# A streaming-encoder block on one core: a ring of small tiles made 64 bytes wider, and the tiles behind it moved

## The chip, the core and the metric

The kernel runs on one core of a Trainium2 chip. The metric is the device time of one execution in microseconds (us); the time before is the median of 3 runs. A duration in nanoseconds is marked ns. The engines are named as in the profile: PE is TensorE (PEld its weight loads), DVE is VectorE, ACT is ScalarE, POOL is GpSimd and SP is SyncE, which only issues transfers.

## What is computed

One layer of an encoder on 256 tokens of width 2048, in float32:

```
x += 1/2 * SwiGLU(norm(x))                  # ffn1: 2048 -> 2 x 5632 -> 2048
h  = norm(x); proj = h @ w_in               # HGRN2, RG-LRU, gates
x += (sig(gate_A) * y_A + sig(gate_B) * y_B) @ w_out
x += CrossAttention(norm(x), norm(mem))     # 4 heads, 256 memory tokens
x += 1/2 * SwiGLU(norm(x))                  # ffn2
out = norm(x)
```

## The kernel before, in words

All large products are done on PE with each operand split in two float32r halves: a high part `h` and a low part `l` of a weight piece, and a high and a low part of the activations. ACT makes the high part (`split`, lines 578 to 580: a copy), DVE the low part (a subtraction). In the two feed-forward stages, ffn1 and ffn2, most products are formed by a scheme of seven products of half-size blocks (`PRODUCTS`, line 1005), for which DVE also makes sums of weight blocks (`td`, `sums_into`) that are split again into a second `h` and a `tl`.

A product of 512 columns is a matmul whose stationary operand (128 columns, loaded into the array before) is a piece of the activations, and whose moving operand is a block of 512 columns of a weight tile. In the profile such a matmul is written `acc<-h,ms`: the moving tile first (`h`, `l`, `tl`), then the stationary one (`ms`, `xh`, `xl`, `xd`, `hidop`, `ops`). In `product` (line 755) of the middle stage it is the other way round, `acc<-ops,h`. Each matmul has its own weight load.

Weight pieces are transferred by SP into tiles of 128 x 2048 float32 (8,192 bytes in each partition). The same kind of tile holds the raw piece, the high and low parts and the sums. There is one ring of them, `big`: ten places that exist for the whole program, and in ffn1 and ffn2 four more from the pool `more` (`FFN_POOLS`, line 870), so 14 places. Between ffn1 and ffn2 the room of these four is used by pools of smaller tiles (`tmp`, `tmp2`, `bias`, `scores`, `extra`, `feature`). The activations' operands stand in 22 tiles of 128 x 1024 (`slots`, 4,096 bytes in each partition). At the start of ffn1 the stationary operands `ms` of the memory's values (`BigOperands`, line 1240) also stand in tiles of the big ring.

A recording layer (`Flow`) takes all operations down, and a planner (`arrange`) sets, from its own table of costs, the order of instructions on every engine and the place in its ring that each tile takes. Neither looks at a tile's address.

Addresses are given out in the order of the pools: constants and the residual, the ten big places, the 22 slots, the pool `small`, and behind it the four places of `more` (in the middle stage the smaller pools). The pool `small` holds statistics of a few columns for each partition. One of its rings, `sst` (class `TokenSquares`, line 872), has two places; each is allocated `PAD` columns wider than the 8 that are used:

```
self.ss = small.tile([P, 8 + PAD], F32, name="sst", tag="sst")[:, :8]
```

Of the kernel before, what the change touches and what calls it, by code (L numbers as in the profile page):

```python
# [36 lines left out]
    VEC[_name] = (_at, _n)  # L37
    _at += _n
NVEC = _at
PAD = 16  # L40


MIXED = {
# [466 lines left out]
def block_kernel(tc: tile.TileContext, xT, xin, memT, mem, vec, gfin, bgate, lruw, wu1, wd1, win, wv,  # L510
# [290 lines left out]
    class Operands:  # L801


        def __init__(self):
            self.tiles = []
            self.cur = None
# [65 lines left out]
    class TokenSquares:  # L872


        def __init__(self):
            self.ss = small.tile([P, 8 + PAD], F32, name="sst", tag="sst")[:, :8]

# [1003 lines left out]
```

## Time and profile before

| | |
|---|---|
| time, median of 3 runs | 2416.99 us (2415.75 to 2417.01) |
| the profiled execution: time, span | 2415.32 us, 2413.5 us |
| granted TensorE clock, mean | 0.999 |
| busy share of the span | PE 99%, PEld 83%, DVE 87%, ACT 67%, POOL 4% |
| moved by DMA | 674.64 MB, mean 280 GB/s |

The span runs from the first to the last instruction; the profiled execution's time is 1.8 us more than its span. Matmuls overlap: one of 512 columns lasts about 390 ns in the records, and the next starts about 230 ns after it. So the time that a matmul costs is read from start to start (below called a step), not from its duration. In the view of instructions in order of time, neighbours of the same kind are merged: a row gives the start, the time from the first one's start to the last one's end, and their number (x16). All instructions stand under one line, L505, the helper that issues everything; so they are told apart by their tiles' names.

### The profile page before, as it was taken

The page shows a single profiled execution, that of the slowest core. Times are in us where ns is not written, and L with a number is a line of the kernel's source. Part 1 is how long each engine was busy: PE and PEld are TensorE (multiplying, and loading weights), DVE is VectorE, ACT ScalarE, POOL GpSimd, SP SyncE. Part 2 cuts the span into 40 slices and gives each one's busy share as a digit, 9 for nine tenths or more (in the row PEclk, how much of TensorE's full clock was granted, in tenths as well). Part 3 has the DMA queues.
Part 4 walks back from the last instruction along what each step waited for, and adds up shares of the span by engine and source line. Part 5 has one row for each costly group of instructions (what it writes and reads, how often), then busy time and mean ns, then how long its engine had stood idle before and what let it go on. Part 6 is the DMA issues. An engine that isn't in the chain of part 4 may idle for free.

```text
span 2413.5 us, 31228 instructions
## 1 busy us (share of the span) xinstructions
PE 2400.6 (99%) x12051; PEld 1994.9 (83%) x12051; DVE 2108.4 (87%) x2348; ACT 1613.6 (67%) x1724; POOL 95.2 (4%) x153
## 2 busy tenths in 40 slices
PE   9999999999999999999999999999999999999998
PEld 8888888888888888888878888888888888888887
DVE  6999999989995998787877988789989999999982
ACT  7866666777778755445774465556777666677776
POOL 0000000000000000000000000000000000000000
PEclk9999999999999999999999999999999999999999
DMA  9767788777766588788888798886898776678786
GB/s 369 253 238 247 256 261 262 252 253 253 246 224 221 212 301 320 286 298 321 295 314 328 288 384 333 322 310 264 323 376 306 262 261 248 229 264 267 264 263 208
DMA packets 101670, 674.64 MB, mean 280 GB/s; under 512 B 11281, under 2 KB 12049, under 8 KB 27153
## 3 DMA queue, kind: packets, MB, share of 16 engines
q1 hardware_dynamic: 79632, 519.47, 57.3%
q0 software_dynamic: 21168, 152.05, 21.3%
q8 instruction: 94, 1.54, 0.2%
q10 hardware_dynamic: 720, 1.13, 0.1%
q14 instruction: 56, 0.45, 0.0%
HBM read 571.94 MB, written 57.67 MB: 261 GB/s over the span
## 4 chain that ended last, share of the span: by engine, by line
PE 97%; ACT 2%; issue 1%; DVE 0%; ACTq 0%
PE acc L505 97%; ACT h L505 1%; ACT L505 0%; ACT r L505 0%; PE warm L505 0%; ACT i L505 0%; DVE l L505 0%; ACT a L505 0%; ACT acc L505 0%; ACT gate L505 0%; ACT x L505 0%; DVE sum L505 0%; DVE tl L505 0%; ACT xc L505 0%; ACT junk L505 0%
## 5 line engine op out<-in xcount | busy, mean ns | idle before, releaser
L505 DVE TENSOR_TENSOR l<-raw,h 128x2048 fp32r<-128x2048 f32 (+2 forms) x411 | 818.7, 1994 | 171.7 <-ACT h L505 115.9
L505 ACT ACTIVATE h<-raw 128x2048 fp32r<-128x2048 f32 (+2 forms) x411 | 686.5, 1675 | 220.9 <-PE acc L505 82.6
L505 ACT ACTIVATE h<-td 128x1024 fp32r<-128x1024 f32 (+1 forms) x278 | 331.0, 1198 | 222.0 <-DVE td L505 194.0
L505 PE MATMUL acc<-h,xl 128*128 128x512 f32 x1218 | 476.3, 391 | 0.0
L505 PE MATMUL acc<-h,xh 128*128 128x512 f32 x1218 | 475.6, 391 | 0.0
L505 DVE TENSOR_TENSOR tl<-td,h 128x1024 fp32r<-128x1024 f32 (+1 forms) x278 | 383.8, 1394 | 11.5 <-ACT h L505 4.8
L505 PE MATMUL acc<-h,hidop 128*128 128x512 f32 x1408 | 357.0, 392 | 0.0
L505 PEld LDWEIGHTS acc<-h,hidop 128*128 128x128 f32 x1408 | 262.6, 188 | 57.8 <-ACT acc L505 0.4
L505 PE MATMUL acc<-h,ops 128*128 128x512 f32 x1192 | 291.1, 392 | 1.6 <-ACT acc L505 1.6
L505 PE MATMUL acc<-ops,h 128*128 128x512 f32 x1152 | 283.8, 393 | 0.0
L505 PEld LDWEIGHTS acc<-h,xh 128*128 128x128 f32 x1218 | 228.5, 188 | 51.1 <-ACT h L505 0.4
L505 PEld LDWEIGHTS acc<-h,xl 128*128 128x128 f32 x1218 | 228.5, 188 | 50.8
L505 PEld LDWEIGHTS acc<-h,ops 128*128 128x128 f32 x1192 | 221.3, 188 | 47.6 <-ACT acc L505 2.9
L505 PEld LDWEIGHTS acc<-ops,h 128*128 128x128 f32 x1152 | 212.1, 188 | 42.9 <-issue 0.9
L505 PE MATMUL acc<-l,hidop 128*128 128x512 f32 x704 | 192.7, 391 | 0.0
L505 PE MATMUL acc<-tl,xh 128*128 128x512 f32 x648 | 178.1, 392 | 0.0
L505 DVE TENSOR_TENSOR td<-raw,td 128x512 f32<-128x512 f32 x252 | 172.0, 683 | 0.8
L505 PE MATMUL acc<-l,xh 128*128 128x512 f32 x570 | 160.7, 391 | 0.0
L505 DVE TENSOR_TENSOR td<-raw 128x1024 f32<-128x1024 f32 x126 | 153.4, 1217 | 6.4 <-DMA raw<-wu 4.2
L505 PEld LDWEIGHTS acc<-ops,l 128*128 128x128 f32 x1152 | 150.8, 191 | 6.7
L505 PEld LDWEIGHTS acc<-l,hidop 128*128 128x128 f32 x704 | 132.0, 188 | 29.2
L505 PE MATMUL acc<-ops,l 128*128 128x256 f32 x1152 | 153.5, 283 | 0.0
(193 smaller groups left out, 2519.7 us busy)
## 6 DMA issues: line engine op xcount, KB each, us to landing
raw<-wu SPq DMA_DIRECT2D x121, 1024.0 KB, 6.8
raw<-wd SPq DMA_DIRECT2D x56, 1024.0 KB, 8.1
made<-wu POOLq DMA_DIRECT2D x46, 1024.0 KB, 6.3
kept<-made POOLq DMA_DIRECT2D x46, 1024.0 KB, 6.6
td<-kept SPq DMA_DIRECT2D x46, 1024.0 KB, 6.9
l<-own POOLq DMA_DIRECT2D x41, 1024.0 KB, 9.4
raw<-win SPq DMA_DIRECT2D x40, 1024.0 KB, 6.1
raw<-wu SPq DMA_DIRECT2D x46, 768.0 KB, 5.6
```

Of the source, the lines that this page charges most:

```text
L505: getattr(op.queue.real, method)(*map(real, args), **{k: real(v) for k, v in kw.items()})
```

## The change

One number: the padding of the ring `sst`.

```diff
-PAD = 16
+PAD = 24
```

The tile `sst` goes from 24 to 32 columns, from 96 to 128 bytes in each partition, and with two places the ring takes 64 bytes more. The order of instructions on PE, DVE, ACT, POOL and SP is the same in both programs, row for row, and each tile takes the same place of its ring. What differs are addresses. In bytes within a partition, and what is left after division by 128:

```
                                  before            after
10 big places         20,096 ..  93,824 (0)     the same (0)
22 slots             102,016 .. 188,032 (0)     the same (0)
sst, two places      192,128 and 192,256 (0)    192,128 (0) and 192,288 (32)
more, 1st big place             192,576 (64)         192,640 (0)
more, 2nd big place             200,768 (64)         200,832 (0)
more, 3rd big place             208,960 (64)         209,024 (0)
more, 4th big place             217,152 (64)         217,216 (0)
middle stage's small pools  from 192,576 (64)   from 192,640 (0)
```

Every block of 512 columns in a weight tile begins a multiple of 2,048 bytes behind the tile's start, and every stationary piece a multiple of 512 bytes, so the remainder by 128 of an operand is that of its tile. The program has 9,517 float32r matmuls of 512 columns. By the remainders of the moving and the stationary operand:

```
moving, stationary    before    after
 0,  0                 7,803    9,517
64,  0                 1,618        0
64, 64                    64        0
 0, 64                    32        0
```

All but the first row lie in ffn1 and ffn2.

## The prediction

> **What bounds the kernel now.** I read the page first, its busy shares and its chain, then PE's waits, then the stages, and at last PE's rows in order of time.
>
> ```profile
> span 2413.5 us, 31228 instructions
> PE 2400.6 (99%) x12051; PEld 1994.9 (83%) x12051; DVE 2108.4 (87%) x2348; ACT 1613.6 (67%) x1724; POOL 95.2 (4%) x153
> PE 97%; ACT 2%; issue 1%; DVE 0%; ACTq 0%
> ```
>
> PE is busy in 2400.6 of 2413.5 us, and the chain that ended last is PE's for 97% of the span. The view of waits, for PE alone, has four rows in all (who waited for whom, us in total, times, longest):
>
> ```profile
> PE acc L505 <- DVE ops L505: 1.9, 1, 1.9
> PE acc L505 <- ACT acc L505: 1.6, 3, 1.0
> PE warm L505 <- DVE ones L505: 1.1, 1, 1.1
> PE acc L505 <- DVE l L505: 0.5, 1, 0.5
> ```
>
> They come to 5.1 us, and no transfer is among them. So PE's own pace is the time: what a matmul costs from start to start, 12,051 times. The two feed-forward stages, in which the moved tiles are used for matmuls, are these two windows (length; busy us and number of instructions of PE, PEld, DVE, ACT, POOL; granted clock, share and rate of DMA):
>
> ```profile
> 0.00:850.00 850.00, 848.93 (x3823) 697.54 (x3824) 766.20 (x858) 611.83 (x632) 28.84 (x39) 1.00 0.76 254
> 1690.00:2414.00 724.00, 715.64 (x3179) 585.69 (x3177) 641.45 (x581) 524.58 (x507) 11.97 (x15) 1.00 0.78 272
> ```
>
> PE is full, at the full clock, and DVE, the next in line, is busy for 766.20 of 850 and 641.45 of 724 us, about 90%.
>
> **What a step costs, by the addresses.** A stretch of ffn1 in order of time (start, us to the last one's end, and at the end the number of matmuls). The step is the difference of two rows' starts, divided by the number.
>
> ```profile
> 12.61 3.79 PE L505 MATMUL acc<-h,ms 128*128 128x512 f32 x16
> 16.23 1.98 PE L505 MATMUL acc<-l,ms 128*128 128x512 f32 x8
> 18.05 3.80 PE L505 MATMUL acc<-h,ms 128*128 128x512 f32 x16
> 21.68 1.97 PE L505 MATMUL acc<-l,ms 128*128 128x512 f32 x8
> 23.50 3.83 PE L505 MATMUL acc<-h,ms 128*128 128x512 f32 x16
> ...
> 28.98 3.79 PE L505 MATMUL acc<-h,ms 128*128 128x512 f32 x16
> 32.61 2.03 PE L505 MATMUL acc<-l,ms 128*128 128x512 f32 x8
> 34.47 3.89 PE L505 MATMUL acc<-h,ms 128*128 128x512 f32 x16
> 38.21 2.00 PE L505 MATMUL acc<-l,ms 128*128 128x512 f32 x8
> 40.04 3.83 PE L505 MATMUL acc<-h,ms 128*128 128x512 f32 x16
> 43.70 2.02 PE L505 MATMUL acc<-l,ms 128*128 128x512 f32 x8
> ```
>
> The built program lists PE's matmuls in the trace's order, so each row's tiles have addresses; I give their remainder by 128, moving operand first.
> - 12.61: `h` and `ms` in big places (0, 0). 16.23 - 12.61 = 3.62 us for 16, 226 ns each. 28.98 (0, 0) likewise: 3.63 us for 16, 227 ns.
> - 34.47: `h` in the fourth place of `more`, `ms` in a big place (64, 0). 38.21 - 34.47 = 3.74 us for 16, 234 ns. 32.61, with `l` in the third place (64, 0): 1.86 us for 8, 233 ns.
> - 18.05 and 21.68: `h` and `l` in the same third and fourth places, but this time `ms` too stands in `more` (64, 64). 3.63 us for 16 and 1.82 us for 8, 227 ns.
> - 40.04: `h` in a big place, `ms` in `more` (0, 64). 3.66 us for 16, 229 ns: in between.
>
> So it isn't the place as such that is slow: the third and fourth places give 227 ns beside a stationary operand of their own remainder, and 233 ns beside one of the other. The two steps are 6.7 ns apart. I read it as two reads of the same memory, the moving block and the next weight load, that get in each other's way when their remainders differ. The end of ffn2 shows the same with other operands:
>
> ```profile
> 2399.08 1.09 PE L505 MATMUL acc<-l,hidop 128*128 128x512 f32 x4
> 2400.01 2.00 PE L505 MATMUL acc<-h,hidop 128*128 128x512 f32 x8
> 2401.84 1.07 PE L505 MATMUL acc<-l,hidop 128*128 128x512 f32 x4
> 2402.75 1.98 PE L505 MATMUL acc<-h,hidop 128*128 128x512 f32 x8
> 2404.56 1.10 PE L505 MATMUL acc<-l,hidop 128*128 128x512 f32 x4
> ```
>
> `l` is in the fourth place of `more`, `h` in a big one. `l` at 2399.08: 0.93 us for 4, 232 ns; `h` at 2402.75: 1.81 us for 8, 226 ns. The rows 32.61 and 2404.56 are the first and the last of the 1,618 matmuls of the kind (64, 0).
>
> Over the whole trace, the steps of that kind, without the 9 over 260 ns that hold a wait, have a mean of 233.25 ns (1,608 steps). The kind (0, 0) in the same two stages has 227.87 ns (4,793 steps under 260 ns). This is above 226.7 because a sixth of them are of 231 ns or more too, for another reason, in runs such as the second here:
>
> ```profile
> 1692.05 1.98 PE L505 MATMUL acc<-l,ops 128*128 128x512 f32 x8
> ...
> 1694.66 3.89 PE L505 MATMUL acc<-h,ops 128*128 128x512 f32 x16
> 1698.38 1.98 PE L505 MATMUL acc<-l,ops 128*128 128x512 f32 x8
> 1700.20 3.79 PE L505 MATMUL acc<-h,ops 128*128 128x512 f32 x16
> 1703.82 1.98 PE L505 MATMUL acc<-l,ops 128*128 128x512 f32 x8
> ```
>
> Both operands of all these rows are at remainder 0, and yet 1694.66 takes 3.72 us for 16, 233 ns, and 1700.20 3.62 us, 226 ns.
>
> **The change part by part.** The order of instructions, the waits and the transfers are the same; only addresses move.
> - *Moving blocks in `more`, 1,618 matmuls.* They become (0, 0). I take the mean of that kind, not its best: 233.25 - 227.87 = 5.38 ns, by 1,617 steps (the last matmul has no step behind it) 8.70 us, all of it on PE and so on the path. At best all of them run at the fast step, 6.67 ns by 1,618: 10.8 us.
> - *The 32 matmuls (0, 64)* have a mean of 230.48 ns now; 2.6 ns by 32 is 0.1 us. *The 64 of kind (64, 64)* have 227.92 ns and gain nothing.
> - *DVE and ACT on the moved tiles.* Operations of one form work on tiles of both remainders today, with durations (min/median/max ns) that leave no room for two kinds:
>
> ```profile
> L505 DVE TENSOR_TENSOR td<-raw,td x252: 676/682/694, 78.4 to 2335.9; 128x512 f32<-128x512 f32 x126
> L505 DVE TENSOR_TENSOR td<-raw x126: 1210/1216/1228, 75.6 to 2330.3; 128x1024 f32<-128x1024 f32 x126
> L505 DVE TENSOR_TENSOR ev<-acc,ev x154: 678/684/694, 115.3 to 2345.0; 128x512 f32<-128x512 f32 x154
> ```
>
>   So nothing, and in the middle stage, whose small pools move too, nothing either: no float32r operand stands there. The second place of `sst` goes to remainder 32; it holds 8 columns and its use is off PE.
> - *Transfers into the moved tiles* could be some hundredths of a us earlier or later; PE has no row that waits for one, so 0.
> - *What is given back.* PE is to go 0.55% faster in stages where DVE is busy for 90%, which makes that 90.5%. PE's waits for DVE and ACT today are 5.1 us in all, so there is room nearly everywhere; I take 0.3 us off.
>
> The sum: 8.70 + 0.1 - 0.3 = 8.5 us. From the profiled execution's span, 2413.5 us, this gives 2405.0 us; that execution's time of 2415.32 us is 1.67 us below the median of the runs. From the median, 2416.99 - 8.5 = 2408.5 us.
>
> **The rivals.** A measurement of this kernel can tell 0.2% from no change, 4.8 us: faster is below 2412.2, slower above 2421.8 us.
>
> *The address doesn't matter to PE*, and the slow steps are of the upper end of the memory, where all four places of `more` lie before and after. Then nothing moves: 2417.0 us. For it: height and remainder go together in 1,618 of the matmuls. Against it: 18.05 and 34.47, the same two places at 227 and at 233 ns. It would need a rule in which a high moving tile beside a low stationary one is slow, with the border between 188,032 and 192,576 bytes. I give it 5%. The Trainium skill (TensorE: Matmul & The Clock Gate, "Step-by-step: what each phase is for") says that the array has two independent read ports, so that loading the next weights takes nothing from the running matmul; by that rule no pair of addresses is dearer than another, and the time stays at 2417.0 us. Its "Back-to-back issue gap" gives 215.8 ns for 512 columns, in that section's own terms for an isolated stream; the trace has 226 and 233 ns, and the difference goes with the pair of addresses, so here the trace speaks against it.
>
> *All in one phase collide.* After the change every large tile of ffn1 and ffn2 has remainder 0, those that DVE and ACT read and write included, of which four in fourteen are out of phase today. If the slow run at 1694.66 comes from such accesses, then the share of slow steps grows. If all 4,841 steps (0, 0) of the two stages went to 233.25 ns as the 1,617 stay there, the cost would be 4,841 x 5.38 ns = 26.0 us: 2443 us. It breaks even when the slow share of the stages' 6,458 steps rises by 8.7 us / (6,458 x 6.67 ns), 20 points over the sixth of today, and is slower than the bound of 0.2% from 31 points. Against it: the row 1700.20, at remainder 0 beside the same work, is fast. 3%. A rise of 8 points would cost 3.4 us and leave 2412.0 us.
>
> *DVE becomes the bound* and PE waits for what it gained: 2412 to 2417 us. At 90% busy against 99%, 2%.
>
> **How the numbers follow.** The forecast, 2408.5 us, has 90%. Its lower end is the 10.8 us of the best case, 2406.2, rounded to 2406.0 us; the upper end is the rise by 8 points, 2412.0 us. I hold nine in ten of the forecast's cases to lie between these, so the range leaves out 2 in 10 together with the rivals. Faster by over 0.2%: the forecast, 0.91 with part of the third rival; within 0.2%: the first rival and the rest of the third, 0.06; slower: 0.03.
>
> **What would show it.** In the changed kernel's rows, 32.61 and 34.47 (their counterparts, `l` x8 and `h` x16) should take 227 ns a step, not 233; the steps of all 1,618 matmuls should have a mean near 228 ns; PE's waits should stay near 5 us; the saving should lie in the two windows of ffn1 and ffn2, about 4.8 us in the first (888 of the matmuls) and 3.9 us in the second (730), and nothing in between. The prediction is wrong if those matmuls still take 233 ns, if steps that were fast become slow, or if PE shows new waits of several us.

## The result, and the profile after

The changed kernel takes 2405.78 us (median of 5 runs, 2404.99 to 2406.69) against 2416.99 us of the kernel before in the same measurement (5 runs, 2415.75 to 2417.28): a ratio of 0.9955 with a 95% interval of 0.9941 to 0.997, that is 2402.7 to 2409.7 us. The medians are 11.2 us apart. The forecast was 2408.5 us: the direction holds, and the size was too small by 2.7 us. The median lies 0.2 us below the lower end of the forecast's range, 2406.0 us, which had been taken for the best case. The profiled execution took 2404.99 us, its span is 10.3 us shorter than before. From the page, the span, the busy shares and the chain that ended last:

```profile
span 2403.2 us, 31228 instructions
PE 2389.4 (99%) x12051; PEld 1998.6 (83%) x12051; DVE 2107.7 (88%) x2348; ACT 1611.8 (67%) x1724; POOL 95.0 (4%) x153
PE 88%; DVE 4%; ACT 4%; issue 2%; DMA 2%; SPq 0%; ACTq 0%; DVEq 0%; POOLq 0%
```

PE's busy time fell by 11.2 us, that of DVE and ACT by 0.7 and 1.8 us. The chain now passes through DVE and ACT for 4% each: followed back from the end, it leaves PE at one of the few steps in which PE waited. PE is still busy for 99%, so this is no new bound. The waits of PE:

```profile
PE acc L505 <- DVE ops L505: 1.9, 1, 1.9
PE acc L505 <- ACT acc L505: 1.6, 3, 1.0
PE warm L505 <- DVE ones L505: 1.1, 1, 1.1
PE acc L505 <- ACT h L505: 0.6, 2, 0.3
PE acc L505 <- DVE l L505: 0.5, 1, 0.5
```

One row is new, 0.6 us for `h`; the sum is 5.7 us, 5.1 before. The two windows of the feed-forward stages:

```profile
0.00:850.00 850.00, 848.38 (x3859) 705.23 (x3860) 772.31 (x866) 618.00 (x638) 29.34 (x40) 1.00 0.76 256
1690.00:2414.00 724.00, 704.91 (x3153) 581.59 (x3151) 636.07 (x576) 518.78 (x501) 11.76 (x15) 1.00 0.78 272
```

In the same 850 us PE gets through 3,859 instructions, before 3,823. The stretch of ffn1 that the prediction read, now:

```profile
12.64 3.79 PE L505 MATMUL acc<-h,ms 128*128 128x512 f32 x16
...
28.96 3.79 PE L505 MATMUL acc<-h,ms 128*128 128x512 f32 x16
32.59 1.98 PE L505 MATMUL acc<-l,ms 128*128 128x512 f32 x8
34.41 3.79 PE L505 MATMUL acc<-h,ms 128*128 128x512 f32 x16
38.03 1.98 PE L505 MATMUL acc<-l,ms 128*128 128x512 f32 x8
39.84 3.79 PE L505 MATMUL acc<-h,ms 128*128 128x512 f32 x16
43.47 1.98 PE L505 MATMUL acc<-l,ms 128*128 128x512 f32 x8
```

Every row of 16 now takes 3.79 us and every row of 8 takes 1.98, at whichever place the tiles stand. 38.03 - 34.41 = 3.62 us for 16, 226 ns a step (234 before). The last rows of the program show the same with `hidop`:

```profile
2391.55 1.07 PE L505 MATMUL acc<-l,hidop 128*128 128x512 f32 x4
2392.45 1.98 PE L505 MATMUL acc<-h,hidop 128*128 128x512 f32 x8
2394.27 1.07 PE L505 MATMUL acc<-l,hidop 128*128 128x512 f32 x4
```

Both programs have the same 12,051 PE instructions in the same order, so each step can be set beside its own counterpart. By the kind that the matmul had before (remainders by 128, moving operand first; stages divided at 850 and 1690 us of the trace before, so that the kind (0, 0) has 4,907 steps here):

```
kind before, stage            steps    mean before -> after    change
(64, 0), ffn1 and ffn2        1,606    233.25 -> 226.89 ns     -10.2 us
(0, 0), ffn1 and ffn2         4,847    227.87 -> 226.97 ns      -4.3 us
(64, 64) and (0, 64)             95                             -0.2 us
steps over 260 ns of these       72                             +1.8 us
warm-up matmuls at the start                                    +0.8 us
middle stage                                                    +1.75 us
all                                                            -10.3 us
```

The second row was not in the forecast. Before, every sixth of these steps was slow (230.5 ns or more: 0.166 of them), after it 0.04. Where the slow ones stood is told by the 256 runs of (64, 0) matmuls. The share of slow steps by place behind the end of such a run, in the profile before:

```
place behind the run     1st    2nd    3rd    4th, 5th    later
share of slow steps      0.05   0.95   0.10     0.86       0.05
```

After the change it is 0.03 to 0.05 at each of these places. So a run of matmuls with an unfavourable pair of addresses left a trail of some three slow steps, though these have a favourable pair of their own. One such trail stands in the prediction's last fence of ffn2: 2400.01, right behind the slow `l`, lasts 2.00 us for 8, and 2402.75, behind a fast `l`, 1.98 us.

Of the middle stage's +1.75 us, about 1.6 us fall on one spot, behind PE's longest wait (1.9 us for `ops` of DVE). The windows after, with the granted clock as the third number from the end:

```profile
1622.00:1624.00 2.00, 1.13 (x6) 1.00 (x7) 2.00 (x5) 0.68 (x2) 0.00 (x0) 1.00 1.04 428
1624.00:1626.00 2.00, 2.00 (x9) 1.71 (x8) 1.83 (x5) 2.00 (x5) 0.00 (x0) 0.54 0.99 403
1626.00:1628.00 2.00, 2.00 (x8) 1.66 (x7) 1.93 (x4) 1.10 (x4) 0.00 (x0) 0.61 0.96 352
```

The windows of the kernel before at the same matmuls:

```profile
1629.00:1631.00 2.00, 1.65 (x9) 1.42 (x10) 2.00 (x4) 1.70 (x4) 0.00 (x0) 1.00 1.04 438
1631.00:1633.00 2.00, 2.00 (x13) 1.75 (x12) 2.00 (x8) 1.91 (x5) 0.00 (x0) 1.00 0.80 245
```

At half the clock a step takes 427 ns for 512 columns and 213 ns for 256; at the full one 233 and 116 ns. The two windows with 0.54 and 0.61 together lost 1.7 us of full clock, so the half clock lasted about 3.4 us. The clock fell at this spot in 4 of the 10 profiled executions of this program's versions (after, `all64`, `more32`, `pad40`) and in none of the other 6, among them versions with the same pairs of addresses as after (`pad56`, `pad88`). So it doesn't go with the pairs of addresses. It isn't spread evenly either. Profiles without this fall have a mean clock of 0.999 over the run, those with it 0.998 or 0.999. A mean of 0.998 stands in 4 of 5 runs of the changed kernel and in 7 of 10 of `more32`, but in 2 of the 49 runs of the kernel before that were measured beside the experiments. What decides it isn't shown.

### The profile page after: what moved, and what is told of

It is laid out like the page before. It is cut to its first block, busy times and chain, and to the rows that moved or that the text cites. A ratio compares the mean times of both kernels' runs of the same rounds, so it can differ in the third digit from the quotient of the medians.

```text
span 2403.2 us, 31228 instructions
## 1 busy us (share of the span) xinstructions
PE 2389.4 (99%) x12051; PEld 1998.6 (83%) x12051; DVE 2107.7 (88%) x2348; ACT 1611.8 (67%) x1724; POOL 95.0 (4%) x153
## 4 chain that ended last, share of the span: by engine, by line
PE 88%; DVE 4%; ACT 4%; issue 2%; DMA 2%; SPq 0%; ACTq 0%; DVEq 0%; POOLq 0%
PE acc L505 88%; DVE tl L505 1%; DVE td L505 1%; ACT h L505 1%; DVE l L505 1%; DMA raw<-wvm 1%; ACT L505 1%; DMA x<-xin 1%; DMA l<-own 0%; ACT xg L505 0%; ACT xh L505 0%; ACT r L505 0%; ACT i L505 0%; DVE ev L505 0%; SPq L505 0%
```

## The experiments

The theory under test: a matmul's step depends on the pair of addresses, moving operand against stationary one, and not on either alone. Its rivals: the moved places are dear by themselves (by their height, or by their own remainder of 64), or any move of them would have mended it. Within the theory it was open what counts: the remainders by 128, as the prediction had it, or something finer. All ratios are against the kernel before, measured beside each version.

Below, "by 128" and "by 256" mean what is left after division by 128 or 256, and a distance such as -64 is the moving operand's address minus the stationary one's, by 256.

**Everything 64 bytes further (`all64`).** `more` goes where the change puts it, and all that lies behind the constants is moved by another 64 bytes, so that all 9,517 matmuls have both operands at remainder 64.

```diff
-PAD = 16
+PAD = 24
...
-    par = const.tile([P, 96], F32, name="par")
+    par = const.tile([P, 112], F32, name="par")
```

> The changed kernel with everything behind the constants 64 bytes further on, so that all 9,517 matmuls are of the pair (64, 64). Theory A: as the changed kernel, 2405.8 us within 1.5 us. Theory B: every one of the 9,517 is slow, 6.4 ns each, 61 us: 2467 us.

2404.51 us (2403.88 to 2404.97), ratio 0.9949 (0.9936 to 0.9961): as the changed kernel. The matmul of `h` in the fourth place of `more` (34.47 before, 3.89 us for 16) takes

```profile
34.14 3.79 PE L505 MATMUL acc<-h,ms 128*128 128x512 f32 x16
```

The mean step in ffn1 and ffn2 is 226.96 ns. An operand's own remainder of 64 costs nothing as long as the other has it too. So the rival that a remainder of 64 is dear by itself falls. The rival of the height has fallen with the changed kernel itself, whose four places lie as high as before and are fast.

**Other distances of the four places (`pad32`, `more96`, `more32`).** `pad32` widens each `sst` by 16 columns against before, which puts `more` at remainder 64 by 128 again, but 128 bytes further.

```diff
-PAD = 16
+PAD = 32
```

> The kernel before with PAD = 32: the four places of more move by 128 bytes and are at remainder 64 again. If the remainder by 128 decides: as before, 2417.0 us within 1.5 us. If the place was bad for another reason, or any move mends it: near 2405.8 us.

2415.56 us (2414.17 to 2417.04), ratio 0.9994 (0.9985 to 1.0003). The gain is gone, so not any move mends it. But these matmuls are not as slow as before: 231.29 ns in the mean, two thirds of them slow, while before 98 in 100 were. The row of `h` in the fourth place, and the one behind it:

```profile
35.32 3.83 PE L505 MATMUL acc<-h,ms 128*128 128x512 f32 x16
38.98 2.02 PE L505 MATMUL acc<-l,ms 128*128 128x512 f32 x8
```

38.98 - 35.32 = 3.66 us for 16, 229 ns (234 before). By their remainders by 128 the two programs are the same; so that remainder doesn't tell all. That the time is hardly better than before's has a second part: the kind (0, 0) of the two stages went up from 227.87 to 228.27 ns, about 1.9 us over 4,863 steps, so here the trails are longer.

`more96` and `more32` widen the second place of `sst` alone, and put `more` 32 bytes below and 32 bytes above the place that the changed kernel gives it (against that kernel):

```diff
-PAD = 24
+PAD = 16; WIDER = {"sst1": 8}
...
-                    x.at = p.at.tile(x.shape, x.dt, name=x.name, tag=f"{x.ring.tag}{i}")
+                    x.at = p.at.tile([P, x.shape[1] + WIDER.get(x.ring.tag + str(i), 0)], x.dt, name=x.name, tag=f"{x.ring.tag}{i}")[:, :x.shape[1]]
```

> The kernel before with the four places of more at remainder 96 instead of 64 (one place of the ring sst is 32 bytes wider): 1,618 matmuls are (96, 0). If the half of 128 bytes in which an operand begins decides (0 to 63 or 64 to 127): as before, 2417 us. If it is the distance, and 64 is the worst: between 2406 and 2417 us.

For `more32` the second line of it reads

```diff
+PAD = 16; WIDER = {"sst1": 24}
```

> The kernel before with the four places of more at remainder 32: 1,618 matmuls are (32, 0). If the half of 128 bytes decides: as the changed kernel, 2405.8 us. If any difference of remainders costs: as before, 2417 us. If it is the distance: in between.

`more96`: 2417.41 us (2415.75 to 2418.19), ratio 1.0001 (0.9991 to 1.0011). `more32`: 2419.57 us (2418.43 to 2420.32), ratio 1.0012 (1.0003 to 1.0021). The row of `h` in the fourth place, first in `more96`, then in `more32`:

```profile
34.60 3.89 PE L505 MATMUL acc<-h,ms 128*128 128x512 f32 x16
```

```profile
34.53 3.90 PE L505 MATMUL acc<-h,ms 128*128 128x512 f32 x16
```

The matmuls with a moving operand in `more` have means of 233.53 and 233.43 ns. A distance of 32 bytes, either way, is as dear as before's 64. So the half of 128 bytes in which an operand begins doesn't decide, and 64 isn't the worst distance. The 2.9 us that `more32` loses against before are mostly in the trails: the kind (0, 0) of the two stages goes from 227.87 to 228.32 ns, and 4,900 steps by 0.45 ns are 2.2 us.

**The other operand moved (`slots64`).** The tenth big place is made 64 bytes wider, with `PAD` as before. Then the 22 slots, which hold the activations, go to remainder 64 and `more` to 0. Against the changed kernel:

```diff
-PAD = 24
+PAD = 16; WIDER = {"big9": 16}
```

(with the same line for `x.at` as above.)

> The four places of more at remainder 0 as in the changed kernel, but the 22 slots, which hold nearly all stationary operands, at 64: 7,737 matmuls are (0, 64), 1,152 of the middle stage (64, 0), 244 (64, 64) and 384 (0, 0). Theory A with both directions alike: 8,889 by 6.4 ns, 57 us over the changed kernel, 2463 us. Theory A with the direction (0, 64) half as dear, as 32 such matmuls of before suggest (230.5 ns): 7,737 by 3.6 ns and 1,152 by 6.4 ns, 35 us: 2441 us. Theory B: only the 1,396 with the moving operand at 64 are slow, 9 us: 2415 us.

2447.06 us (2446.29 to 2448.09), ratio 1.0125 (1.0111 to 1.0139): 30 us slower than before, with the same instructions. None of the three forecasts (2463, 2441 and 2415 us) was met. The 6,115 matmuls of ffn1 and ffn2 with a moving weight block at 0 and a stationary operand at 64 have a mean of 233.34 ns, 97 in 100 slow. The prediction had taken the kind (0, 64) for half as dear as (64, 0), from 32 matmuls at 230.48 ns. In the middle stage 1,055 matmuls of the opposite kind, moving 64 and stationary 0, have 229.63 ns. So the direction counts, and again a remainder by 128 doesn't say which is which: (64, 0) was dear in before, (0, 64) here. The last rows of this program, to be set beside those after:

```profile
2433.54 1.09 PE L505 MATMUL acc<-l,hidop 128*128 128x512 f32 x4
2434.47 2.03 PE L505 MATMUL acc<-h,hidop 128*128 128x512 f32 x8
2436.34 1.10 PE L505 MATMUL acc<-l,hidop 128*128 128x512 f32 x4
```

2436.34 - 2434.47 = 1.87 us for 8, 234 ns; after, 1.82 us, 227 ns.

**The pair by itself (`pairs`).** A kernel of its own that computes nothing of the reference: PE alone, runs of 24 matmuls of 512 columns, each run with the operands shifted by some bytes (`mv` for the moving one, `st` for the stationary one) and with an unshifted run (`even`) between them.

```
for word, m, s in CONFIGS:
    run(acc("even"), 24, 0, 0)
    a = acc(word)
    run(a, 24, m // 4, s // 4)
```

Here `m` and `s` are the bytes by which the moving and the stationary operand are shifted.

> This kernel computes nothing of the reference: it runs matmuls of 512 columns alone on PE, 24 in a row for each pair of remainders by 128 of the moving (mv) and the stationary (st) operand, and runs of 1 to 16 odd matmuls (moving at 64, stationary at 0) followed by 24 even ones (0, 0). Theory A, the pair decides: 24 matmuls at mvsixtyfour and at stsixtyfour take 233 ns a step, bothsixtyfour and mvonetwentyeight 227 ns. Theory B, the moving operand's own remainder (or its height) decides: mvsixtyfour and bothsixtyfour 233 ns, stsixtyfour 227 ns. After the odd runs: if an odd run leaves a trail, the 24 even steps behind it hold two or three slow ones (231 to 236 ns), about 20 ns over 24 steps, whatever the length of the odd run; if the slow even steps of the kernel come from accesses of the other engines, there are none here, since these are idle.

It took 392.1 us. Each run begins another accumulation, and PE breaks off there for two steps of some 450 and 340 ns, so the rows are only compared with each other:

```profile
64.51 5.77 PE L65 MATMUL mvsixtyfour<-mv,st 128*128 128x512 f32 x24
70.34 5.74 PE L65 MATMUL even<-mv,st 128*128 128x512 f32 x24
...
99.54 5.71 PE L65 MATMUL mvonetwelve<-mv,st 128*128 128x512 f32 x24
...
111.11 5.86 PE L65 MATMUL mvonetwentyeight<-mv,st 128*128 128x512 f32 x24
...
157.93 5.86 PE L65 MATMUL stsixtyfour<-mv,st 128*128 128x512 f32 x24
...
216.53 5.75 PE L65 MATMUL bothsixtyfour<-mv,st 128*128 128x512 f32 x24
```

DVE and ACT stand still here, and the rows still differ: so it is between PE's two operands, no other engine needed. Both shifted by 64 costs nothing (5.75 against 5.74), the stationary one alone 0.12 us in 24, the moving one alone by 64 bytes only 0.03, and by 128 bytes 0.12. The last two are not as expected: the moving one at 64 was to be as dear as the stationary one, and a shift of 128 is no shift by 128. Where both are shifted, by 96 and 32 bytes, the 24 take 5.79 us, close to the 64 alone: the difference counts. What a run leaves behind couldn't be seen here, since each begins with a break.

**The difference, step by step (`steps`).** The same without breaks: one accumulation through the whole kernel, nothing of the reference, the stationary operand at a multiple of 256 bytes, the moving one shifted against it by the number in its name (`minussixtyfour` is a shift by 448, which is -64 by 256), always with 24 unshifted matmuls (`zero`) in between. At the end 1, 2, 4, 8 and 16 matmuls at -64, each time with 24 unshifted behind them.

```
DIFFERENCES = [("sixteen", 16), ("thirtytwo", 32), ("sixtyfour", 64), ("ninetysix", 96), ("onetwelve", 112),
               ("onetwentyeight", 128), ("oneninetytwo", 192), ("twofiftysix", 256), ("threetwenty", 320),
               ("threeeightyfour", 384), ("minussixtyfour", 448), ("minusthirtytwo", 480)]
```

> This kernel computes nothing of the reference: one long accumulation on PE alone, whose moving tile changes. Tile zero begins at the same address modulo 512 as the stationary tile st; the others begin the named number of bytes after it (36 matmuls each, 24 of zero between). Theory C, the difference of the two addresses within 512 bytes decides: zero and onetwelve 227 ns a step; sixteen to ninetysix and onetwentyeight to minusthirtytwo between 229 and 234 ns, minussixtyfour at 233 ns and sixtyfour at 229 ns. If the length is 256 and not 512 bytes, twofiftysix takes 227 ns and threetwenty and threeeightyfour behave as sixtyfour and onetwentyeight. Theory A, remainders by 128: onetwentyeight, twofiftysix and threeeightyfour take 227 ns. At the end, 1 to 16 matmuls of minussixtyfour and 24 of zero behind them, three times each, without a break: a trail of two or three slow steps shows as about 15 to 20 ns in the 24 steps of zero beside 24 undisturbed ones (5.44 us); without a trail they take 5.44 us.

It took 303.97 us. PE's rows in order of time, first the differences, then the ends of two short runs:

```profile
52.50 8.42 PE L72 MATMUL acc<-sixtyfour,st 128*128 128x512 f32 x36
60.76 5.65 PE L72 MATMUL acc<-zero,st 128*128 128x512 f32 x24
66.25 8.58 PE L72 MATMUL acc<-ninetysix,st 128*128 128x512 f32 x36
...
80.14 8.47 PE L72 MATMUL acc<-onetwelve,st 128*128 128x512 f32 x36
88.45 5.65 PE L72 MATMUL acc<-zero,st 128*128 128x512 f32 x24
93.94 8.55 PE L72 MATMUL acc<-onetwentyeight,st 128*128 128x512 f32 x36
102.33 5.62 PE L72 MATMUL acc<-zero,st 128*128 128x512 f32 x24
...
121.65 8.32 PE L72 MATMUL acc<-twofiftysix,st 128*128 128x512 f32 x36
129.81 5.60 PE L72 MATMUL acc<-zero,st 128*128 128x512 f32 x24
135.25 8.42 PE L72 MATMUL acc<-threetwenty,st 128*128 128x512 f32 x36
...
162.84 8.56 PE L72 MATMUL acc<-minussixtyfour,st 128*128 128x512 f32 x36
171.24 5.62 PE L72 MATMUL acc<-zero,st 128*128 128x512 f32 x24
...
190.57 0.39 PE L72 MATMUL acc<-minussixtyfour,st 128*128 128x512 f32 x1
190.80 5.62 PE L72 MATMUL acc<-zero,st 128*128 128x512 f32 x24
196.26 0.39 PE L72 MATMUL acc<-minussixtyfour,st 128*128 128x512 f32 x1
```

From start to start: 256 takes 129.81 - 121.65 = 8.16 us for 36, 226.7 ns, and the unshifted run behind it 5.44 us for 24, 226.7 ns as well. 128 takes 8.39 us, 233 ns; -64 takes 8.40 us, 233 ns. 320, which is 64 by 256, takes 8.26 us, 229 ns, and 64 the same (60.76 - 52.50 = 8.26 us); 384 takes 233 ns, as 128. So the period is 256 bytes. All differences, each by its row:

```
moving minus stationary, by 256:   0     16    32    64    96   112   128   -64   -32
step, ns:                         227   231   234   229   234   231   233   233   233
```

At 112 the expectation, 227 ns, was missed: 88.45 - 80.14 = 8.31 us for 36, 231 ns. It came from `pairs`, where the moving operand shifted by 112 bytes cost nothing (5.71 us). Why the two kernels differ there stays open.

And the trail: after a single matmul at -64, 24 unshifted ones take 196.26 - 190.80 = 5.46 us, undisturbed ones (129.81) 5.44 us. It is 0.02 us after 1, 2, 4, 8 and 16 of them alike, with steps of 226, 236, 228, 233, 231 ns and then 227 ns. So it needs no other engine either, and at -64 the length of the run doesn't matter. After +64 it is longer, 66.25 - 60.76 = 5.49 us, so 0.05 us; that fits the dearer kind (0, 0) of `pad32`. In before, 256 runs by 0.02 us are 5.1 us, near the 4.3 us that the kind (0, 0) gained.

**128, 256 and 512 bytes (`pad40`, `pad56`, `pad88`).** The whole program, with `more` moved on from where the changed kernel has it:

```diff
-PAD = 24
+PAD = 40
```

> The kernel before with PAD = 40: the four places of more are at remainder 0 by 128, like all others, but 128 bytes off the others modulo 512. Theory A, remainder by 128: as the changed kernel, 2405.8 us within 1.5 us. Theory C: the 1,618 matmuls take 232 to 233 ns, as before, 2416 us within 2 us.

```diff
-PAD = 24
+PAD = 56
```

> The kernel before with PAD = 56: the four places of more are 256 bytes off the others modulo 512. Theory A: 2405.8 us. Theory C with 256 bytes: 2405.8 us. Theory C with 512 bytes: a few ns more for each of the 1,618 matmuls, 2410 to 2418 us.

```diff
-PAD = 24
+PAD = 88
```

> The kernel before with PAD = 88: the four places of more are 512 bytes further on than in the changed kernel. Theories A and C, with 256 or 512 bytes, all say 2405.8 us within 1.5 us; another time would mean a longer period still.

In `pad40` all 9,517 matmuls have remainder 0 by 128, as after, and 1,650 of them a difference of 128 by 256. It takes 2415.33 us (2414.19 to 2416.34), ratio 0.9994 (0.9985 to 1.0002): the gain is gone. The 1,618 with a moving operand in `more` have a mean of 232.1 ns. `pad56`: 2404.56 us (2404.25 to 2405.07), 0.995 (0.9938 to 0.9963). `pad88`: 2404.7 us (2403.94 to 2407.11), 0.9953 (0.9939 to 0.9966). `h` in the fourth place, in `pad40`, `pad56` and `pad88`:

```profile
34.04 3.90 PE L505 MATMUL acc<-h,ms 128*128 128x512 f32 x16
```

```profile
34.48 3.79 PE L505 MATMUL acc<-h,ms 128*128 128x512 f32 x16
```

```profile
34.49 3.79 PE L505 MATMUL acc<-h,ms 128*128 128x512 f32 x16
```

This settles it on the program itself: equal by 256 is fast, equal by 128 isn't enough. It also sorts the earlier runs. All big places and slots before have remainder 128 by 256 and `more` is 64 (192,576): moving minus stationary is -64, dear; its 32 matmuls (0, 64) are +64, and took 230.48 ns. In `pad32` `more` is 192: +64, cheaper, as measured. In `slots64` the weights are 128 and the slots 192: -64 again where the weights move, and +64 in the middle stage where the slots' operand moves. The changed kernel puts `more` at 128 (192,640), like the rest. None of the versions with all pairs equal (`all64`, `pad56`, `pad88`) beats the changed kernel by more than the measurement can tell.

## Why the prediction was right, and where it wasn't

- *What bounds the kernel* was right: PE's steps are the time. The sum of PE's steps fell by 10.3 us, the span as well.
- *The pair of addresses* was the right cause. The rival that the address doesn't matter falls with the result, and so does its form that the upper end of the memory is slow: the four places lie there in the changed kernel too, and higher still in `pad56` and `pad88`, and are fast. The Trainium skill (TensorE: Matmul & The Clock Gate, "Step-by-step: what each phase is for") says that loading the next weights takes nothing from the running matmul. The runs don't bear out that the pair is therefore free: with PE alone the step is 227 to 234 ns by the difference of the two start addresses. A collision of two reads in the memory, as the prediction had it, is a reading that fits; no run shows the reads themselves, nor whether it is the matmul's own weight load or the next one's that counts, since neighbours nearly always have the same pair.
- *"I give their remainder by 128"* was the wrong measure. It is the difference by 256, with its sign (`pad40`, `steps`). The forecast survived because the change makes the operands equal by both. That was luck: the same rule would have forecast `pad40` as fast as the changed kernel, 10 us off.
- *"5.38 ns, by 1,617 steps 8.70 us"* was too small: the steps measured -10.2 us. The target was taken as the mean of the kind (0, 0), 227.87 ns, and that mean held the slow steps that the change removes. The best case, 10.8 us, took the fast step for them, but was no bound either: it had no term for the steps of the next point.
- *"a sixth of them are of 231 ns or more too, for another reason"* is the step that failed. In ffn1 and ffn2 three quarters of these were the trails of the very matmuls that the change moves: -4.3 us that the sum didn't have. The row chosen for it, 1694.66, misled: read step by step it has one of 314 ns, two of 232 and 231, and then 13 of 226 or 227. It stands behind a break by small matmuls (`vt,x`), which the mean of 16 spread over the row; its counterpart after has the same steps. From this one place the prediction took a cause for all.
- *"I take 0.3 us off"* was too small. Steps over 260 ns cost 1.8 us more, 0.6 us of it as waits that the profile names; the rest of what was given back, 0.8 us at the warm-up and 1.6 us at half the clock, doesn't go with the pairs of addresses. The warm-up's row of 32 matmuls lasts 5.38 to 6.63 us over the ten profiles, whatever the addresses. In all, the profiled execution gained 14.7 us and gave back 4.4; forecast were 8.8 and 0.3. That the two errors partly cancel, so that the sum came out within 3 us, is luck as well.
- *Where the saving lies* was right, its size too small: 6.65 us in ffn1 and 5.41 us in ffn2 (forecast 4.8 and 3.9), none in between. *DVE and ACT* gained nothing from the addresses, as said: their busy times moved by 0.7 and 1.8 us of some 2100 and 1600; and DVE didn't become the bound. *All in one phase collide* fell: the share of slow steps sank from 0.166 to 0.04.

What stays open: why -64 costs more than +64, and why a trail has the form that it has. The middle stage's slow steps (0.16 of them, before and after) stand mostly within eight steps of a break in the row of matmuls, about nine in ten of 457 before. In `pairs` the unshifted steps behind a break look alike, even where the run before the break had an equal pair too (behind `bothsixtyfour` 231, 231, 236, 228, 233 and 231 ns, then 227), so a break may leave a trail as well; it wasn't tested further.

## What to carry to other kernels

Where PE is the bound by matmuls like these (512 columns, float32r, a weight load for each), look up the start addresses of their two operands, and lay the tiles so that they are equal by 256 bytes; padding one small tile can be worth half a per cent, and one wrong widening (`slots64`) costs more than twice as much. If a mean is taken as the target for what a change will reach, ask first whether the slow members of that mean are neighbours of the very instructions that change. A rule read from one program's addresses holds only for the remainders that occur there: test it at the next larger period before using it.

## What the runs showed of the hardware

- The step of a float32r matmul of 512 columns, with its own weight load, is 226.7 ns when both operands start at the same address by 256 bytes, and 229 to 234 ns at the other distances tried in `steps`; one matmul at -64 leaves about 20 ns in the steps behind it, and a run at +64 about 50 ns.
- For 256 columns it is not the same: in `slots64` the 1,152 matmuls `acc<-ops,l`, with the moving operand at +64, have a mean step of 117.5 ns; before, with equal starts, it is 120.5 ns. The sum over them is 3.5 us less in a kernel that was 30 us slower. A version with these alone at +64 wasn't tried.
- Behind a wait of 1.9 us PE's granted clock fell to one half for about 3.4 us (0.54 and 0.61 in the mean of two windows of 2 us; a step of 427 ns) in 4 of 10 profiled executions, and not in the other 6, which have the same wait.
